# Moving a depthwise convolution's taps, a modulation product and some operands between the engines of a fused two-layer decoder trunk

## The chip, the cores and the metric

One core of a Trainium2 chip runs the whole network as one program. The metric is the time on the device in microseconds (us); the time of a kernel is the median of several runs. One further execution of each kernel is recorded by the hardware profiler. The engines are named as in the profile: PE multiplies matrices (PEld is its weight load), DVE is the vector engine, ACT the scalar engine, POOL the GpSimd engine, and SP only issues DMAs.

## What is computed

Sequence length S = 1024, width D = 1024, feed-forward width F = 2816, two layers, all in fp32. Layer 0 mixes tokens with a convolution module, layer 1 with a pooling mixer; each is followed by a gated feed-forward block.

```python
c_act = silu(c)
for i in range(2):
    mod = c_act @ ada_w[i] + ada_b[i]                # six vectors of 1024
    sh_m, sc_m, g_m, sh_f, sc_f, g_f = split(mod, 6)
    h = rms_norm(x, norm_mix_g[i]) * (1 + sc_m) + sh_m
    y = conformer_conv(h) if i == 0 else multiscale_pool(h)
    x = x + (1 + g_m) * y
    h = rms_norm(x, norm_ffn_g[i]) * (1 + sc_f) + sh_f
    x = x + (1 + g_f) * ((silu(h @ w_gate) * (h @ w_up)) @ w_down)
return rms_norm(x, final_g)

def conformer_conv(h):
    a, g = split(h @ w1 + b1, 2)
    u = a * sigmoid(g)
    u = causal_depthwise_conv(u, w_dw, width=31) + b_dw
    return silu(layer_norm(u)) @ w2 + b2
```

## The kernel before

Activations lie transposed: channels on the 128 partitions (eight tiles of 128 channels, p or k = 0 to 7), tokens along the free axis, in two chunks A and B of 512 tokens. Each product is taken from three matmuls of 512 columns on split operands (`products`, L410): high times high, high times low, low times high, so a weight and an activation exist as a "hi" and a "lo" tile. The low part of a streamed weight is made in `load_weight` (L394): SP loads the raw tile of 512 KB, ACT writes the high part and a negated copy (two instructions on 128x1024), and POOL issues a second DMA of the same bytes that adds into the negated copy (L406). Five weight buffers and three raw buffers rotate.

PE's instructions run in the order of the code. The order on the other engines is made by a scheduler when the program is built; on the chip each engine and each DMA queue runs its list strictly in that order. Work beside the products is cut into generators (`Task`, `Taps`) that `pace()` moves forward at every twelfth or twenty-fourth matmul, as far as a model clock for each engine allows; the prices in `PRICES` set how many steps DVE ("V") and POOL ("G") get. `finish()` and `need()` move what is left of a task at once and stand for the places where the next products need its result.

Stages of layer 0, in PE's order:

- "first": the products of the first four tiles of w1 for chunk A, tile by tile of the input, while the first norm is made. For this DVE computes `sh_m` and `sc_m` as dot products of 1024 elements (`ada_dot`, L308), two for each of the eight tiles.
- The other tiles of w1 for A (outputs "a" and "g") and for B. `conv_glu` (L565) makes u from a pair of outputs, and u's last 30 columns are kept in `uhalo` for B. Meanwhile the taps of the convolution for A run: for tiles 0 to 6 a `Taps` task (L636) deals its 31 taps out, DVE taking multiply-adds into a PSUM bank "ca", POOL taking adds into "pa" of products "pr" that ACT makes. Tile 7 goes over PE: `pe_taps` (L617) multiplies by 128x128 diagonal matrices, one for each tap, split into hi and lo, which ACT makes from an identity (`diagonals`, L605; 62 instructions); its u is split by `split_u`, into two slots of chunk B's pool of u tiles.
- In the same stretch `ada_columns` (L352) computes four modulation vectors (`g_m`, `sh_f`, `sc_f`, `g_f`; j = 2 to 5) on PE, 32 rounds, one for each loaded tile "adaw" of 512 KB from `adan`; a round is eight matmul records and comes at a pace point, at least LOAD["load"] = 2.5 us of the model clock behind the round before. Two buffers hold these tiles, filled from SP's queue.
- `finish` of A's taps, then two tiles of w1 for B (HOLD_LN = 2) beside the layer norm of A (`layer_norm_silu`, L706: sum over tiles, mean on PE, centring, squares, variance, then vhi and vlo).
- "y": the products with w2 for A (`conv_out`, eight tiles, 192 matmuls), the sum of squares of the new x, one more tile of w1 for B, then the norm of the feed-forward block for A, which needs `sc_f` and `sh_f`.
- The feed-forward blocks ("gate", "up", "dn"), with B's taps beside A's block, and layer 1 in the same manner.

A's activations (hhi, hlo, vhi, vlo, mxhi, mxlo) lie in sixteen slots of 512 columns, got by `slot` (L232).

Of the kernel before, what the change touches and what calls it, by code (L numbers as in the profile page):

```python
# [9 lines left out]
F32 = mybir.dt.float32  # L10
# [6 lines left out]
P = 128  # L17
# [27 lines left out]
PE_TAPS = (7,)  # L45
DIAGS = 8
OUT_B = 3
LOAD = {"load": 2.5, "slow": 18.0, "next": 4.0}
# [20 lines left out]
class Chunk:  # L69
# [9 lines left out]
    "G": {"": (0.15, 0.0021, 0.06), "tensor_scalar": (0.2, 0.0009, 0.06), "memset": (0.06, 0.0, 0.0), "tensor_copy": (0.2, 0.0, 0.0)},  # L79
    "S": {"": (0.1, 0.00083, 0.09)},  # L80
}

# [25 lines left out]
def trunk(ctx, tc, xT, c, vec, ada, adan, w1f, w1, w2, wgu, wdn, wpl, out):  # L108
# [51 lines left out]
    def nm(s):  # L160
        uid[0] += 1
        return f"{s}_{uid[0]}"
# [69 lines left out]
    def slot(ch, name, dt=F32R):  # L232

        return slots.tile([P, ch.n], dt, tag=f"s{ch.i}", name=nm(name))
# [223 lines left out]
    class Squares:  # L458


        def __init__(self, ch, psum=False):
            self.ch, self.acc, self.psum = ch, None, psum

        def add(self, k):
            ch = self.ch
            if self.acc is None:
                self.acc = bank("acc") if self.psum else temp(ch.n, "acc", 2)
                S_.activation(self.acc, x[ch.i][k], AF.Square)
            else:
                sq = temp(ch.n)  # L470
                S_.activation(sq, x[ch.i][k], AF.Square)
                was = self.acc
                if self.psum and k == KT - 1:
                    self.acc = temp(ch.n, "acc", 2)
                V_.tensor_tensor(self.acc, was, sq, op=ADD)
# [89 lines left out]
    def conv_glu(ch, p, ba, bg):  # L565
        u = st["u", ch.i, p]
        sg = temp(ch.n)
        S_.activation(sg, bg, AF.Sigmoid, bias=V("conv_b1", KT + p))
        V_.scalar_tensor_tensor(u[:, HALO:], ba, V("conv_b1", p), sg, op0=ADD, op1=MUL)
        if ch.i == 0:  # L570
            G_.tensor_copy(uhalo[:, p, :], u[:, ch.n : ch.n + HALO])

    def conv_in(*todo):

        def emit(take):
            got = {}
            for each in todo:
                if each is None:
                    finish(T["norm_b"])
                    continue  # L580
                ch, p = each
                conv_u(ch, p)
                wts = got.setdefault(p, [])
                b = [bank("a"), bank("g")]
                for i in range(2):
                    if len(wts) == i:
                        wts.append(take())
                    for k in range(KT):
# [4 lines left out]
                if ch.i == 0 and p in PE_TAPS:  # L593
                    split_u(p)
                elif ch.i == 0:
                    T["taps", 0, p] = Taps(A, p)
        tiles = list(dict.fromkeys(e[1] for e in todo if e))
        unit(emit, *[w1[p, i] for p in tiles for i in range(2)])

    def split_u(p):  # L600

        u = st["u", 0, p]
        hi, lo = st["us", p] = [wslot(B, name, F32R) for name in ("uhi", "ulo")]
        S_.copy(hi, u)
        either(A.width).tensor_tensor(lo, u, hi.bitcast(F32), op=SUB)  # L605

    def diagonals(p, js):

        def make():
            wt = wts.tile([P, 2, D], F32R, tag="w", name=nm("diag"))  # L610
            for i, j in enumerate(js):
                for part, w in enumerate((vecs[:, _COLS["conv_wdw"] + j * KT + p :][:, :1], wlow[:, j, p - PE_TAPS[0] : p - PE_TAPS[0] + 1])):
                    S_.activation(wt[:, part, i * P : i * P + P], ident, AF.Copy, scale=w)
            return wt
        return make

    def pe_taps(p):  # L617

        groups = [range(j, min(j + DIAGS, CW)) for j in range(0, CW, DIAGS)]
        us = []  # L620
        for i, js in enumerate(groups):
            def emit(take, i=i, js=js):
                if i == 0:
                    st["tap", p] = bank("tap")
                b, wt = st["tap", p], take()
                for q, j in enumerate(js):
                    products(b, wt, q, [v[:, j : j + A.n] for v in st["us", p]], j == 0, j == CW - 1)
                    if q % 4 == 3:
                        pace()
                if i == len(groups) - 1:  # L630
                    S_.activation(st["u", 0, p][:, HALO:], b, AF.Identity, bias=V("conv_bdw", p))
                    st["taps", 0][p] = True
            us.append((emit, diagonals(p, js)))
        return us

    class Taps:  # L636
# [5 lines left out]
        def __init__(self, ch, p):  # L642
            self.ch, self.p, self.done, self.urgent = ch, p, False, False
            self.next, self.acc, self.part, self.busy = 0, None, None, 0
            tasks.append(self)

        def step(self, e):
# [6 lines left out]
            if self.next < CW - 1:  # L654
                if e == "V" and self.acc is None and sum(isinstance(t, Taps) and t.acc is not None for t in tasks) >= 2:
                    return False
                if e == "G":
                    if self.acc is None and self.part is None and sum(isinstance(t, Taps) and t.part is not None for t in tasks) >= 2:
                        return False
                    if self.next >= CW - 3:  # L660
                        return False
# [21 lines left out]
            if e != "V":  # L683
                return False
            if self.part is not None:
                V_.tensor_tensor(self.acc, self.part, self.acc, op=ADD)
            d = u[:, HALO : HALO + n]
            V_.scalar_tensor_tensor(d, d, w(CW - 1), self.acc, op0=MUL, op1=ADD)
# [17 lines left out]
    def layer_norm_silu(ch):  # L706
# [293 lines left out]
    rstd_last = V_.last.ins.name  # L1000
    h_a = st["h", 0] = [(slot(A, "hhi"), slot(A, "hlo")) for _ in range(KT)]
    fb = [bank("first") for _ in range(BANKS)] + [spare_bank("first") for _ in range(2 * FIRST - BANKS)]
    for k in range(KT + 1):
        if k < KT:
            if k:
                w = ada_pair(k)
                ada_dot(w[:, 1], 0, 1, k)
                tc.add_manual_dep(V_.last.ins, t_last, edge, reason="behind the first norm")
        if k > 0:
            dot = V_.last.ins.name  # L1010
            V_.scalar_tensor_tensor(h_a[k - 1][1], t, mod[:, k - 1 : k], h_a[k - 1][0].bitcast(F32), op0=ADD, op1=SUB)
            if k < KT:
                tc.add_manual_dep(V_.last.ins, dot, edge, reason="the scalar engine's part takes that long")
            for q in range(2 * FIRST):
                products(fb[q], wt, q, h_a[k - 1], k == 1, k == KT)
        if k < KT:
            ada_dot(w[:, 0], 0, 0, k)
            if k == 0:
                tc.add_manual_dep(V_.last.ins, rstd_last, edge, reason="behind the first norm")
# [10 lines left out]

    wdw = V("conv_wdw", 0, CW * KT).rearrange("p (j k) -> p j k", k=KT)[:, :, PE_TAPS[0] : PE_TAPS[-1] + 1]
    whigh = cst.tile([P, CW, len(PE_TAPS)], F32R, name="whigh")
    wlow = cst.tile([P, CW, len(PE_TAPS)], F32, name="wlow")
    S_.copy(whigh, wdw)
    G_.tensor_tensor(wlow, wdw, whigh.bitcast(F32), op=SUB)
# [38 lines left out]
    def ada_first(take):  # L1074
        T["ada", 0] = Task(ada_columns((2, 3, 4, 5)), False, 0)
        T["ada", 0].free = True
    unit(ada_first)
    def norm_first():
        squares = Squares(B, True)
        for k in range(KT):  # L1080
            squares.add(k)
            yield
# [16 lines left out]
    unit(lambda take: finish(*(T["taps", 0, p] for p in range(KT) if p not in PE_TAPS)))  # L1099
# [9 lines left out]
    unit(lambda take: stretch.__setitem__(0, STRETCH))  # L1109
# [97 lines left out]
```

## Time and profile before

| | us |
|---|---|
| median of 3 runs (lowest, highest) | 1869.29 (1868.43, 1871.13) |
| the profiled execution | 1870.55 |
| span of its trace | 1868.8 |
| PE busy | 1819.3 (97%) |
| PE weight loads busy | 1479.8 (79%) |
| DVE busy | 970.0 (52%) |
| ACT busy | 982.7 (53%) |
| POOL busy | 626.7 (34%) |
| DMA | 382.31 MB, mean 205 GB/s |

Times inside the trace count from the start of its span. A busy share is an average over very different stages: "first" ends at 69 us, the convolution stage with the product "y" runs up to about 335 us, and the rest is feed-forward. The chain of waits names for each moment the instruction that set the end; the windows view gives, for stretches of 20 us, each engine's busy time with the number of its instructions in brackets, then the clock that PE was granted (1.00 is full speed), the busy share of the DMA engines and the rate in GB/s.

### The profile page before, as it was taken

Reading aid. Unit: us, or ns where it says so; the run is one execution under the profiler, and the core shown is the slowest. Engines: PE = TensorE matmul, PEld = TensorE weight load, DVE = VectorE, ACT = ScalarE, POOL = GpSimd, SP = SyncE. Lnnn points to the kernel's source line nnn. Section 1 sums busy time; section 2 is a strip of 40 time slices with the busy share of each in tenths; the row PEclk is TensorE's granted clock in tenths of the full one; section 3 lists DMA queues with packets and bytes.
Section 4 is the critical chain, followed back from the end, with each engine's and each line's share of the span. In section 5 each row is a group of like instructions: output and inputs, shape, how many; then the busy total and the mean of one; then the engine's idle time right before and its main releaser. Section 6 shows DMA issues by size and latency. Waiting matters only on the chain.

```text
span 1868.8 us, 22009 instructions
## 1 busy us (share of the span) xinstructions
PE 1819.3 (97%) x8197; PEld 1479.8 (79%) x8197; DVE 970.0 (52%) x1489; ACT 982.7 (53%) x1302; POOL 626.7 (34%) x670
## 2 busy tenths in 40 slices
PE   6899989999999999999999999999999999999997
PEld 5666678888888888877888888888888888888886
DVE  8699753998876236486633223644432243322225
ACT  3566766866656454554553445644534454444443
POOL 4387721878753211273211111421111111111111
PEclk9999989999999999999999999999999999999998
DMA  7968558898897988999887887878888879788782
GB/s 281 289 189 225 150 121 203 205 227 221 210 235 187 237 221 194 262 266 271 232 207 180 198 198 182 193 180 208 188 187 193 195 175 250 178 202 198 181 196 68
DMA packets 106844, 382.31 MB, mean 205 GB/s; under 512 B 11633, under 2 KB 13809, under 8 KB 106738
## 3 DMA queue, kind: packets, MB, share of 16 engines
q0 software_dynamic: 43488, 158.35, 46.1%
q1 hardware_dynamic: 62160, 221.51, 34.4%
q8 instruction: 64, 1.05, 0.2%
q10 hardware_dynamic: 1090, 1.05, 0.2%
q14 instruction: 42, 0.34, 0.1%
HBM read 376.67 MB, written 4.19 MB: 204 GB/s over the span
## 4 chain that ended last, share of the span: by engine, by line
PE 89%; DMA 5%; DVE 4%; POOL 1%; issue 1%; ACT 0%; SPq 0%; DVEq 0%; POOLq 0%
PE gate L124 24%; PE dn L124 24%; PE up L124 24%; PE y L124 6%; PE a L124 3%; PE g L124 3%; PE first L124 2%; DMA adaw<-in_adan_dram 2%; DMA adaw<-in_ada_dram 2%; DVE adaw L102 1%; DVE acc L102 1%; PE ada L124 1%; DVE t L102 1%; PE tap L124 1%; PE rstd L124 1%
## 5 line engine op out<-in xcount | busy, mean ns | idle before, releaser
L102 ACT CAST w<-raw 128x1024 fp32r<-128x1024 f32 x312 | 325.9, 1045 | 509.3 <-issue 300.4
L124 PE MATMUL gate<-hhi,w 128*128 128x512 f32 x1408 | 451.2, 390 | 1.5 <-DVE x L102 1.4
L124 PE MATMUL up<-hhi,w 128*128 128x512 f32 x1408 | 451.4, 390 | 0.0
L124 PE MATMUL dn<-ghi,w 128*128 128x512 f32 (+1 forms) x1440 | 446.0, 387 | 1.7 <-DMA w<-in_wdn_dram 1.7
L406 POOL DMA_DIRECT2D w<-in_wgu_dram x176 | 154.7, 879 | 759.4 <-ACT w L102 739.9
L102 DVE SCALAR_TENSOR_TENSOR x<-dn,gains,x 128x512 f32<-128x512 f32 (+1 forms) x360 | 261.4, 735 | 113.6 <-PE dn L124 113.3
L102 ACT ACTIVATE w<-raw 128x1024 fp32r<-128x1024 f32 x302 | 318.7, 1055 | 0.0
L124 PEld LDWEIGHTS dn<-ghi,w 128*128 128x128 f32 x1440 | 267.8, 187 | 60.0 <-DMA w<-in_wdn_dram 2.2
L124 PEld LDWEIGHTS gate<-hhi,w 128*128 128x128 f32 x1408 | 264.3, 188 | 57.9 <-DVE x L102 2.6
L124 PEld LDWEIGHTS up<-hhi,w 128*128 128x128 f32 x1408 | 264.3, 188 | 54.8
L102 DVE TENSOR_TENSOR t<-t,up 128x512 f32<-128x512 f32 x86 | 59.0, 686 | 475.1 <-PE up L124 446.7
L124 PE MATMUL dn<-glo,w 128*128 128x512 f32 (+1 forms) x720 | 278.5, 387 | 0.0
L124 PE MATMUL gate<-hlo,w 128*128 128x512 f32 x704 | 274.3, 390 | 1.4 <-DVE hlo L102 1.4
L124 PE MATMUL up<-hlo,w 128*128 128x512 f32 x704 | 273.9, 389 | 0.0
L102 POOL TENSOR_TENSOR pa<-pa,pr 128x512 f32<-128x512 f32 x165 | 232.0, 1496 | 27.2 <-ACT pr L102 24.4
L102 DVE SCALAR_TENSOR_TENSOR ca<-u,vecs,ca 128x512 f32<-128x512 f32 x255 | 176.1, 746 | 0.7
L124 PEld LDWEIGHTS dn<-glo,w 128*128 128x128 f32 x720 | 135.1, 188 | 28.3 <-issue 0.2
L124 PEld LDWEIGHTS gate<-hlo,w 128*128 128x128 f32 x704 | 132.1, 188 | 29.6 <-DVE hlo L102 2.3
L406 POOL DMA_DIRECT2D w<-in_wdn_dram x88 | 78.5, 892 | 225.8 <-ACT w L102 223.8
L124 PEld LDWEIGHTS up<-hlo,w 128*128 128x128 f32 x704 | 132.1, 188 | 27.2
L102 ACT ACTIVATE t<-gate 128x512 f32<-128x512 f32 x86 | 51.2, 595 | 156.9 <-PE gate L124 151.7
L102 DVE SCALAR_TENSOR_TENSOR adaw<-adaw,cact 128x1024 f32<-128x1024 f32 x64 | 108.2, 1693 | 42.6 <-DMA adaw<-in_ada_dram 42.6
(139 smaller groups left out, 1799.1 us busy)
## 6 DMA issues: line engine op xcount, KB each, us to landing
raw<-in_wgu_dram SPq DMA_DIRECT2D x176, 512.0 KB, 6.9
w<-in_wgu_dram POOLq DMA_DIRECT2D x176, 512.0 KB, 8.0
raw<-in_wdn_dram SPq DMA_DIRECT2D x88, 512.0 KB, 5.4
w<-in_wdn_dram POOLq DMA_DIRECT2D x88, 512.0 KB, 9.0
adaw<-in_ada_dram SPq DMA_DIRECT2D x48, 512.0 KB, 7.4
raw<-in_w_dram SPq DMA_DIRECT2D x36, 512.0 KB, 5.2
w<-in_w_dram POOLq DMA_DIRECT2D x34, 512.0 KB, 8.4
adaw<-in_adan_dram SPq DMA_DIRECT2D x32, 512.0 KB, 5.5
```

The source lines that it names most:

```text
L102: self.last = self.order(getattr(self.eng, name)(out, *args, **kw))
L124: last_mm[0] = nc.tensor.matmul(out, lhsT, rhs, start=start, stop=stop).ins.name
L406: order(nc.gpsimd.dma_start(low if len(src.shape) == 2 else low.rearrange("p (a b) -> p a b", a=src.shape[1]), src, accum_op=ADD))
```

## The change

Taps. `PE_TAPS` becomes a map: tile 7 has all 31 taps on PE, and tile 6 has its last 8 there; the other 23 stay with DVE and POOL, and its `Taps` task ends by adding the PSUM bank that PE filled. The diagonals are no longer made by ACT. They are laid out on the host in DRAM (`wdg`), five tiles of 128x1024 (eight taps each), and come through `load_weight` like every other weight. The splits of u now lie in A's slots, with two zero columns ahead, and a tap moves its shift partly to the output: a tap at distance s writes from column 2*(s//2) on, so it has fewer columns. For that each slot of A has 514 columns, and every tile that `slot` returns starts at its third column.

Modulation. `ada_columns` keeps j = 2 and 3 (16 rounds), paced by 4.0 in place of 2.5. `sc_f` and `g_f` (j = 4 and 5) become dot products on DVE, two tasks of eight, started when the layer norm of A is done, that is ahead of "y", each paced by 3.5; `sc_f` has to be finished behind "y".

Operands and order. The running sum of A's layer norm lies in PSUM until its last step, and so does the first tile's t in "first". Tile 7's u is made in place in PSUM and split from there. `uhalo` is written by DVE (ACT for tile 7) in place of POOL. In "first" the low part of tile 0 comes ahead of the dots of tile 1. The squares for B's first norm are issued one step ahead of their sums. POOL's price per element in the planner goes from 0.0021 to 0.0026 until the feed-forward block starts.

```diff
-PE_TAPS = (7,)
+PE_TAPS = {6: 8, 7: CW}
-LOAD = {"load": 2.5, "slow": 18.0, "next": 4.0}
+LOAD = {"load": 4.0, "slow": 18.0, "next": 4.0, "dots": 3.5}
-    "G": {"": (0.15, 0.0021, 0.06), ...
+    "G": {"": (0.15, 0.0026, 0.06), ...
+def tap_groups(p):
+    todo = list(range(CW - 1, CW - 1 - PE_TAPS[p], -1))
+    return [todo[i : i + DIAGS] for i in range(0, len(todo), DIAGS)]
...
     def slot(ch, name, dt=F32R):
-        return slots.tile([P, ch.n], dt, tag=f"s{ch.i}", name=nm(name))
+        return slot_after(ch, name, dt)[:, 2 - 2 * ch.i :]
+    def slot_after(ch, name, dt=F32R):
+        return slots.tile([P, ch.n + 2 - 2 * ch.i], dt, tag=f"s{ch.i}", name=nm(name))
...
-    def ada_task(l, js):
+    def ada_task(l, js, pause=None):
...
-                yield "next" if lax[0] else "slow"
+                yield pause or ("next" if lax[0] else "slow")
...
+        if ch.i == 0 and PE_TAPS.get(p) == CW:
+            V_.scalar_tensor_tensor(ba, ba, V("conv_b1", p), sg, op0=ADD, op1=MUL)
+            hi, lo = st["us", p] = [slot_after(A, name) for name in ("uhi", "ulo")]
+            for part in (hi, lo):
+                G_.memset(part[:, :2].bitcast(F32), 0.0)
+            S_.copy(hi[:, 2:], ba)
+            V_.tensor_tensor(lo[:, 2:], ba, hi[:, 2:].bitcast(F32), op=SUB)
+            S_.copy(uhalo[:, p, :], ba[:, ch.n - HALO :])
+            return
         V_.scalar_tensor_tensor(u[:, HALO:], ba, V("conv_b1", p), sg, op0=ADD, op1=MUL)
         if ch.i == 0:
-            G_.tensor_copy(uhalo[:, p, :], u[:, ch.n : ch.n + HALO])
+            V_.scalar_tensor_tensor(uhalo[:, p, :], ba[:, ch.n - HALO :], V("conv_b1", p), sg[:, ch.n - HALO :], op0=ADD, op1=MUL)
...
     def split_u(p):
-        u = st["u", 0, p]
-        hi, lo = st["us", p] = [wslot(B, name, F32R) for name in ("uhi", "ulo")]
+        u = st["u", 0, p][:, HALO - 2 :]
+        hi, lo = st["us", p] = [slot_after(A, name) for name in ("uhi", "ulo")]
         S_.copy(hi, u)
-        either(A.width).tensor_tensor(lo, u, hi.bitcast(F32), op=SUB)
-    def diagonals(p, js):
...
-                    S_.activation(wt[:, part, i * P : i * P + P], ident, AF.Copy, scale=w)
+        either(A.n).tensor_tensor(lo, u, hi.bitcast(F32), op=SUB)
     def pe_taps(p):
...
-                    products(b, wt, q, [v[:, j : j + A.n] for v in st["us", p]], j == 0, j == CW - 1)
+                    o = (CW - 1 - j) // 2 * 2
+                    i0 = 2 - (CW - 1 - j) % 2
+                    products(b[:, o:], wt, q, [v[:, i0 : i0 + A.n - o] for v in st["us", p]], j == CW - 1, j == CW - PE_TAPS[p])
...
+                    else:
+                        T["taps", 0, p].other = b
-            us.append((emit, diagonals(p, js)))
+            us.append((emit, wdg[sum(len(tap_groups(q)) for q in PE_TAPS if q < p) + i]))
...
-            if e != "V":
+            if e != "V" or self.awaits and self.other is None:
                 return False
...
+            if self.awaits:
+                if self.part is not None:
+                    V_.tensor_tensor(d, self.part, self.acc, op=ADD)
...
+                V_.tensor_tensor(d, d, self.other, op=ADD)
...
-        acc = temp(n, "acc", 2)
+        acc = None
...
+            was = vs[0] if k == 1 else acc
+            if k == KT - 1 or ch.i and acc is None:
+                acc = temp(n, "acc", 2)
+            elif acc is None:
+                acc = bank("acc")
-            V_.tensor_tensor(acc, vs[0] if k == 1 else acc, vs[k], op=ADD)
+            V_.tensor_tensor(acc, was, vs[k], op=ADD)
...
+            if k == 1:
+                tc.add_manual_dep(dots[0], low_last, edge, reason="behind the first values")
...
-            t = temp(A.n)
+            t = temp(A.n) if k else first_t
...
-        T["ada", 0] = Task(ada_columns((2, 3, 4, 5)), False, 0)
+        T["ada", 0] = Task(ada_columns((2, 3)), False, 0)
...
     need("ln_a")
+    unit(lambda take: [T.__setitem__(("ada", 0, j), ada_task(0, (j,), "dots")) for j in (5, 4)])
     sq_a = Squares(A)
     conv_out(A, sq_a, lambda take: [now(columns_done(*g)) for g in held_back])
+    unit(lambda take: finish(T["ada", 0, 4]))
     unit(lambda take: T.__setitem__("norm_a", Task(norm(A, 0, True, ("h", 0), squares=sq_a), True)))
```

More of the change, by code (lines that the diff above doesn't have):

```diff
@@ L107, in trunk @@
 @with_exitstack
-def trunk(ctx, tc, xT, c, vec, ada, adan, w1f, w1, w2, wgu, wdn, wpl, out):
+def trunk(ctx, tc, xT, c, vec, ada, adan, w1f, w1, wdg, w2, wgu, wdn, wpl, out):
     nc = tc.nc
@@ L1007, in trunk @@
                 ada_dot(w[:, 1], 0, 1, k)
-                tc.add_manual_dep(V_.last.ins, t_last, edge, reason="behind the first norm")
+                if k > 1:
+                    tc.add_manual_dep(V_.last.ins, t_last, edge, reason="behind the first norm")
+                dots = [V_.last.ins]
         if k > 0:
@@ L1079, in norm_first @@
         squares = Squares(B, True)
-        for k in range(KT):
-            squares.add(k)
+        for k in range(KT + 1):
+            if k < KT:
+                squares.square(k)
+            if k > 1:
+                squares.sum(k == KT)
             yield
@@ L1098, in trunk @@
     unit(lambda take: finish(T["ada", 0]))
-    unit(lambda take: finish(*(T["taps", 0, p] for p in range(KT) if p not in PE_TAPS)))
+    unit(lambda take: finish(*(T["taps", 0, p] for p in range(KT) if PE_TAPS.get(p, 0) < CW)))
     for p in rest[len(rest) - HOLD - HOLD_LN : len(rest) - HOLD]:
@@ L1182 @@
     up = np.stack([tiles(np.asarray(ffn_w_up)[l], NF) for l in range(DEPTH)])
+    taps = np.asarray(conv_wdw)[0].reshape(CW, KT, P)
+    groups = [(p, js) for p in sorted(PE_TAPS) for js in tap_groups(p)]
+    diag = np.zeros((len(groups), P, DIAGS, P), np.float32)
+    for i, (p, js) in enumerate(groups):
+        for q, j in enumerate(js):
+            diag[i, range(P), q, range(P)] = taps[j, p]
     arrays = {
```

84 lines of the change are left out of this document (44 added, 40 removed).

## The prediction

> **What bounds the kernel now.** I read the page first, then the windows of 20 us, then the waits and the chain, last the groups of DVE, ACT and POOL inside the convolution stage. The page:
>
> ```profile
> span 1868.8 us, 22009 instructions
> ...
> PE   6899989999999999999999999999999999999997
> ...
> q0 software_dynamic: 43488, 158.35, 46.1%
> q1 hardware_dynamic: 62160, 221.51, 34.4%
> ```
>
> The second row is PE's busy tenths in 40 slices: it is busy throughout, so most of the span is its own matmuls, and a change pays where slices fall under 9, or where matmuls go or grow. The last two rows are the DMA queues with their packets, MB and share of the DMA engines' time. The windows show these places (busy us and instructions of PE, PEld, DVE, ACT, POOL, then clock, DMA share, GB/s):
>
> ```profile
> 80.00:100.00 20.00, 15.67 (x77) 10.34 (x78) 10.91 (x18) 10.34 (x16) 9.15 (x9) 0.83 0.97 274
> ...
> 160.00:180.00 20.00, 17.13 (x93) 11.28 (x93) 15.70 (x20) 10.20 (x16) 14.67 (x13) 0.91 0.87 224
> ...
> 220.00:240.00 20.00, 14.32 (x60) 10.20 (x59) 9.99 (x14) 9.20 (x13) 11.06 (x12) 0.90 0.80 189
> 240.00:260.00 20.00, 18.59 (x77) 14.97 (x76) 14.80 (x34) 12.85 (x18) 4.45 (x6) 0.84 0.31 64
> ...
> 300.00:320.00 20.00, 20.00 (x94) 16.70 (x93) 5.96 (x16) 11.31 (x14) 2.92 (x4) 1.00 0.88 199
> ```
>
> And PE's waits (us in total, times, longest):
>
> ```profile
> PE ada L124 <- DMA adaw<-in_adan_dram: 10.6, 6, 5.2
> ...
> PE mean L124 <- DVE acc L102: 4.7, 1, 4.7
> ```
>
> Full speed is about 90 matmuls per 20 us (fifth row). Behind each idle piece the clock is below 1.00: 0.83 and 0.91 cost up to (0.17 + 0.09) x 20 = 5.2 us behind the waits for "adaw" tiles, 0.90 and 0.84 likewise 5.2 us around the layer norm. The chain (start, duration, what) gives the prices:
>
> ```profile
> 140.67 2.95 PE g L124 x12
> 143.62 0.57 PE ada L124 x8
> ...
> 147.14 2.72 PE a L124 x12
> ...
> 236.91 2.09 PE mean L124 x2
> ...
> 268.28 43.52 PE y L124 x192
> ...
> 320.86 0.91 PE rstd L124 x8
> ```
>
> Twelve matmuls take 2.72 us (226.7 ns each), but 2.95 behind a round "ada", which itself is 0.57: a round costs PE 0.80. The layer norm's mean comes at 236.9, "y" starts at 268.3, it lasts 43.5, and the norm behind it has its rstd at 320.9 + 0.9 = 321.8.
>
> **(a) The start of "first".** DVE's list puts two dots ahead of the first low part:
>
> ```profile
> 18.81 0.74 DVE L102 SCALAR_TENSOR_TENSOR t<-x,gains,rstd 128x512 f32<-128x512 f32 x1
> 19.47 2.71 DVE L102 SCALAR_TENSOR_TENSOR adaw<-adaw,cact 128x1024 f32<-128x1024 f32 x1
> ...
> 22.42 0.73 DVE L102 SCALAR_TENSOR_TENSOR hlo<-t,mod,hhi 128x512 fp32r<-128x512 f32 x1
> ```
>
> and PE's list then has
>
> ```profile
> 23.21 0.79 PE L124 MATMUL first<-hlo,w 128*128 128x512 f32 x1 [2.05 <-DVE hlo L102]
> ```
>
> The x2 row is 2.71 us. With the dots behind, the low part waits only for ACT's hhi and can come at 20.4 instead of 22.4; both dots now stand ahead of tile 1's t, but PE has 24 matmuls (5.4 us) of tile 0 to cover them. I take -1.5; bounds -2.0 and 0, since DVE is nearly saturated behind it. t in PSUM, the reordered squares and `uhalo` move work of under a microsecond between engines beside PE and get nothing; uncovered, eight writes of 30 columns would cost DVE some 2 us.
>
> **(b) PE's work up to the end of the taps.** Sixteen of 32 rounds go: 16 x 0.80 = -12.8. Eight taps add 24 matmuls. A tap's price comes from these two rows of PE's timeline; between them start 30 matmuls:
>
> ```profile
> 224.89 0.63 PE L124 MATMUL tap<-uhi,diag 128*128 128x512 f32 x2
> ...
> 231.86 0.39 PE L124 MATMUL tap<-uhi,diag 128*128 128x512 f32 x1
> ```
>
> (231.86 - 224.89)/30 = 0.232, so +5.6; the shortened outputs take back 3 x 474 columns, 0.6: +5.0. Of the waits for "adaw" (10.6 us in 6) and their clock (I take 3.5 of the 5.2), those behind 150 us (the windows from 160 and from 220) lie in the half of the rounds that is removed, and the remaining loads are asked for about half as often, so I leave 2 us of them: -12.1. Bounds: -14 (all gone) and -6 (the early ones stay, as first loads still meet the weights of the next tiles). Sum (b): -19.9.
>
> **(c) The layer norm of A.** PE gets to its mean some 20 us sooner, so A's taps have to be done sooner too. In the convolution stage (60 to 236 us) these groups count:
>
> ```profile
> L102 DVE SCALAR_TENSOR_TENSOR ca<-u,vecs,ca 128x512 f32<-128x512 f32 x121 | 83.7, 747 | 0.6
> L102 DVE TENSOR_TENSOR acc<-acc,u 128x512 f32<-128x512 f32 x5 | 7.2, 1445 | 0.1
> L102 DVE TENSOR_TENSOR acc<-acc,t 128x512 f32<-128x512 f32 x7 | 4.9, 698 | 10.5 <-ACT t L102 10.3
> L102 DVE TENSOR_TENSOR ca<-pa,ca 128x512 f32<-128x512 f32 x7 | 4.8, 688 | 10.6 <-POOL pa L102 10.6
> L102 POOL TENSOR_TENSOR pa<-pa,pr 128x512 f32<-128x512 f32 x75 | 100.6, 1434 | 17.9 <-ACT pr L102 17.0
> L406 POOL DMA_DIRECT2D w<-in_w_dram x17 | 15.8, 928 | 24.0 <-ACT w L102 21.4 <-issue 2.2 <-POOL pa L102 0.4
> L102 ACT CAST w<-raw 128x1024 fp32r<-128x1024 f32 x18 | 18.8, 1045 | 26.2 <-PE g L124 11.8 <-PE a L124 7.9 <-PE tap L124 6.4
> L102 ACT ACTIVATE w<-raw 128x1024 fp32r<-128x1024 f32 x17 | 18.0, 1058 | 0.0
> L102 ACT ACTIVATE diag<-ident,vecs 128x128 fp32r<-128x128 f32 x31 | 12.0, 388 | 0.3 <-PE a L124 0.3
> L102 ACT ACTIVATE diag<-ident,wlow 128x128 fp32r<-128x128 f32 x31 | 12.0, 388 | 0.0
> ```
>
> DVE waits 10.6 us for POOL's sums and 10.5 for ACT's squares; POOL waits 17.9, nearly all for "pr" of ACT, and 24.0 for ACT's w ahead of its DMA issues. ACT spends 2 x 12.0 us on 62 diagonal pieces, and "pr" waits in the same list. The 62 pieces go. Five weights come in: on ACT 5 x (1.045 + 1.058) = 10.5 us, net -13.5; on POOL five issues of 0.93, +4.6, each of which may also wait for ACT's w with POOL's adds queued behind it; on SP five raw loads, between the others. In the planner a POOL add now costs 0.15 + 512 x 0.0026 = 1.48 us, near the measured 1.434 instead of 1.23, so POOL gets some 12 adds fewer than its 75 (17 us less), and DVE, with eight taps fewer to share, about four more (3 us). The sum in PSUM should bring the five "acc" additions from 1.445 to about 0.70: -3.7 on DVE. Without DVE's waits for POOL and ACT (21 us) and with the work above the taps would end some 25 us sooner, the mean standing at about 212 where it stands at 236.9. So PE's wait for the mean (4.7 us), the one ahead of the variance and their slow clock (10 us together) should not grow: I take -6. Bounds: -10, and +12 if the taps move by only 8 us. The split of tile 6 waits for A's last products to free slots; it is needed only at "tap", two tiles later.
>
> **(d) Sixteen dots beside "y".** DVE is nearly free there (5.96 of 20), so the dots themselves (two took 2.71 us in the row of (a)) are covered. The loads are not: DMA is at 0.88. By the queue rows a weight takes 0.524/158.35 of 46.1% for its second DMA and 0.524/221.51 of 34.4% for its raw one, of 1868.8 us: 2.85 + 1.52 = 4.37 us of all engines for each 5.44 of PE, and a pair of dots adds 3.04. Together 7.4 per 5.44: DMA becomes the bound. Landing times:
>
> ```profile
> adaw<-in_ada_dram SPq DMA_DIRECT2D x48, 512.0 KB, 7.4
> w<-in_w_dram POOLq DMA_DIRECT2D x34, 512.0 KB, 8.4
> 831.19 14.43 DMA adaw<-in_ada_dram
> ```
>
> Two buffers mean two dots for each landing. DMA is emptier just ahead of "y" (0.31 at 240 to 260), so I estimate four to six dots in its first third, then two for each 8 to 9 us (7.4 and a dot): the last of sixteen at about 62 us behind the start of "y", when rstd is ready at 321.8 - 268.3 = 53.5. `sc_f` needs the last or next to last: +7 (a short idle costs clock too). Late next: SP's list is in order, so raw weights wait behind a load without a buffer, and the first gate and up weights come late by about the same; that lies in the same wait. Bounds: 0, if the planned pace holds (a pair per 5.44 us ends at 44), and +30, if landings stay near 14.4.
>
> [...]
>
> **(e) A's slots.** Every operand in a slot of A now starts two columns behind its slot's start, and the slots are 514 columns apart. That looks free, but PE's time per matmul differs between operands of equal size:
>
> ```profile
> 386.52 5.44 PE up L124 x24
> 391.96 10.99 PE dn L124 x48
> 402.94 5.44 PE gate L124 x24
> ```
>
> "gate" takes 5.44/24 = 226.7 ns, "dn" 10.99/48 = 229.0, from tiles of 542 columns read at their start, and the taps, which start anywhere in such a tile, 232.3. A's slots feed 2736 matmuls: first 192, a and g 192, y 192, gate and up 2 x 1056, the pooling mixer's y 48. Nothing hides them. Bounds: 0 at gate's price, 2736 x 5.6 ns = 15.3 at the taps'; between, 6.3 at dn's. I take 15.3, since only the taps start off their tile's start.
>
> [...]
>
> **Sum.** -1.5 - 19.9 - 6 + 7 + 15.3 = -5.1. The span is 1868.8, the profiled execution about 1.8 above it, and that one 1.3 above the median of 1869.3, so 1869.3 - 5.1 = 1864.
>
> **Rivals.** 1, the slots and the dots cost nothing: -27.4, 1842. For it: gate's own price, and a pace that ends at 44 us; against: the tap rows and DMA at 0.88. 2, slower: `sc_f` arrives late. The place is the wait for the norm behind "y"; if landings stay near 14.4 us, two dots for each, sixteen need 115 us; even if the last third speeds up once PE stands still, the norm waits some 30 us: -5.1 + 23 = +18, 1887. It decides against the change from a wait of about 12 us on. For it: two loads in flight only, SP's order; against: the median of 7.4. 3, the taps end only 8 us sooner, because five more POOL issues wait for ACT with its adds behind them: (c) is +7 to +12 instead of -6, total about +10, 1879. For it: POOL's 24.0 us; against: ACT's relief. 4, PE's taps of tile 6 relieve nobody, as DVE's last addition waits for PE's bank: worth eight taps at most, inside (c).
>
> **How the numbers follow.** A measurement of this kernel tells about 0.2% (3.7 us) from no change. Forecast 0.45, of which 0.33 faster, 0.07 within, 0.05 slower; rival 1, with what lies between it and the forecast, 0.22, faster; rival 2 0.16, slower; rival 3 0.14, of which 0.02 faster, 0.01 within, 0.11 slower; anything else 0.03, 0.01 faster, 0.02 slower. Together faster 0.58, within 0.08, slower 0.34. The forecast's own range is 1852 to 1873; out to rival 1 and into rival 2 it is 1843 to 1883.
>
> **What would show it.** (a) the first low matmul near 21 instead of 23.2. (b) sixteen rounds of "ada", few waits for adan, the last tap matmul near 211 instead of 232. (c) "y" starting near 240; if DVE or POOL still ends its last tap past 225, (c) is wrong. (d) the feed-forward norm starting more than 54 us behind y's start, its last dot being what it waits for; no wait there makes it wrong. (e) gate on A at 5.5 to 5.6 us per 24 while B stays at 5.44; 5.44 for both makes it wrong. A loss inside the feed-forward blocks other than (e) would be outside this prediction.

## The result and the profile after

The changed kernel takes 1870.99 us (median of 12 runs, 1867.6 to 1876.35) where the kernel before takes 1869.2 beside it (12 runs, 1865.73 to 1872.33): a ratio of 1.0009, with a 95% interval of 0.9999 to 1.0019. No difference can be told. The forecast of 1864 lay 7 us too low; 1871 is inside its own range and the wide one, but the gain that was forecast isn't there, and "no difference" had been given a chance of 0.08 only.

Two rows of PE's timeline in the kernel before show where the span can be cut: the first matmul of "y" for A and the first "dn" (start and duration in us, engine, line, operation, output and inputs, shapes).

```profile
268.11 0.39 PE L124 MATMUL y<-vhi,w 128*128 128x512 f32 x1
...
359.05 0.39 PE L124 MATMUL dn<-ghi,w 128*128 128x512 f32 x1
```

The same two of the changed kernel, whose span is 1869.4 us:

```profile
238.76 0.49 PE L131 MATMUL y<-vhi,w 128*128 128x512 f32 x1
...
346.16 0.39 PE L131 MATMUL dn<-ghi,w 128*128 128x512 f32 x1
```

| us | before | after | difference |
|---|---|---|---|
| to the first matmul of "y" | 268.1 | 238.8 | -29.4 |
| from there to the first "dn" | 90.9 | 107.4 | +16.5 |
| from there to the end of the span | 1509.8 | 1523.2 | +13.5 |
| span | 1868.8 | 1869.4 | +0.6 |

So the convolution stage won 29 us, and two other stretches gave them back. The waits of PE after the change (us in total, times, longest) show the first line of the table: the 10.6 us for "adaw" and the 4.7 for the mean are nearly gone.

```profile
PE ada L131 <- DMA adaw<-in_adan_dram: 2.2, 3, 1.8
...
PE mean L131 <- DVE acc L109: 1.7, 1, 1.7
```

The windows show the second: at 280 to 320 PE, which was full beside "y" before, is idle for 9 us and its clock is at 0.86 and 0.89.

```profile
260.00:280.00 20.00, 20.00 (x87) 16.20 (x86) 8.73 (x14) 10.72 (x14) 3.36 (x4) 1.00 1.05 306
280.00:300.00 20.00, 14.53 (x62) 11.86 (x61) 8.84 (x15) 8.72 (x11) 2.74 (x4) 0.86 0.99 288
300.00:320.00 20.00, 16.24 (x63) 11.90 (x63) 16.63 (x35) 9.13 (x13) 3.68 (x9) 0.89 0.63 187
```

DVE's timeline there, where a bracket gives the idle time and what ended it, names the cause:

```profile
293.36 1.22 DVE L109 SCALAR_TENSOR_TENSOR adaw<-adaw,cact 128x1024 f32<-128x1024 f32 x1 [1.81 <-DMA adaw<-in_ada_dram]
...
294.51 0.75 DVE L109 SCALAR_TENSOR_TENSOR x<-t,gains,x 128x512 f32<-128x512 f32 x1
...
300.47 1.22 DVE L109 SCALAR_TENSOR_TENSOR adaw<-adaw,cact 128x1024 f32<-128x1024 f32 x1 [3.47 <-DMA adaw<-in_ada_dram]
...
301.62 0.17 DVE L109 TENSOR_SCALAR var<-var 128x4 f32<-128x4 f32 x1
...
307.67 1.23 DVE L109 SCALAR_TENSOR_TENSOR adaw<-adaw,cact 128x1024 f32<-128x1024 f32 x1 [1.93 <-DMA adaw<-in_ada_dram]
...
308.82 2.72 DVE L109 SCALAR_TENSOR_TENSOR t<-x,gains,rstd 128x512 f32<-128x512 f32 x4
```

The norm's first "t" starts at once behind the sixteenth dot, and that dot had to wait for its load. The rows above it show more than the forecast had seen: DVE ran its list in order, so an update of x (294.51) and the variance's first step (301.62) also stand behind a dot that waits for DMA, 1.81 and 3.47 us; ACT had made the update's t by 291.4, 3.1 us before. The groups of the stretch from 240 to 310 us, first DVE's dots (busy us, mean ns, then DVE's idle time ahead of them), then the DMA issues (KB, median us from issue to landing):

```profile
L109 DVE SCALAR_TENSOR_TENSOR adaw<-adaw,cact 128x1024 f32<-128x1024 f32 x16 | 19.6, 1223 | 26.3 <-DMA adaw<-in_ada_dram 26.3
```

```profile
adaw<-in_ada_dram SPq DMA_DIRECT2D x14, 512.0 KB, 7.4
```

The dots cost DVE 19.6 us; their loads cost it 26.3 us of waiting. The third line of the table is seen in the chain of waits: "gate" on a slot of A takes 5.61 us, on a slot of B, far behind, 5.44 as before.

```profile
323.89 5.61 PE gate L131 x24
...
346.32 10.99 PE dn L131 x48
...
1478.97 5.44 PE gate L131 x24
```

### The profile page after: what moved, and what is told of

The parts are those of the page before. It is cut to its first block, busy times and chain, and to the rows that moved or that the text cites. A ratio compares the mean times of both kernels' runs of the same rounds, so it can differ in the third digit from the quotient of the medians.

```text
span 1869.4 us, 21783 instructions
## 1 busy us (share of the span) xinstructions
PE 1826.0 (98%) x8085; PEld 1481.9 (79%) x8085; DVE 990.9 (53%) x1528; ACT 968.0 (52%) x1240; POOL 614.8 (33%) x662
## 3 DMA queue, kind: packets, MB, share of 16 engines
q8 instruction: 64, 1.05, 0.2%
q10 hardware_dynamic: 1090, 1.05, 0.2%
## 4 chain that ended last, share of the span: by engine, by line
PE 82%; DVE 10%; DMA 6%; issue 1%; ACT 1%; SPq 0%; POOL 0%; DVEq 0%
PE gate L131 24%; PE up L131 24%; PE dn L131 24%; DMA adaw<-in_ada_dram 5%; DVE ca L109 4%; PE y L131 4%; PE first L131 3%; DVE adaw L109 1%; DVE acc L109 1%; PE g L131 1%; PE a L131 1%; DVE x L109 1%; DVE t L109 1%; DMA adaw<-in_adan_dram 1%; DVE hlo L109 1%
## 5 line engine op out<-in xcount | busy, mean ns | idle before, releaser
L109 ACT CAST w<-raw 128x1024 fp32r<-128x1024 f32 x317 | 331.0, 1044 | 508.2 <-issue 303.8
L109 ACT ACTIVATE w<-raw 128x1024 fp32r<-128x1024 f32 x307 | 323.9, 1055 | 0.0
L109 POOL TENSOR_TENSOR pa<-pa,pr 128x512 f32<-128x512 f32 x156 | 222.9, 1545 | 13.6 <-ACT pr L109 10.9
L109 DVE SCALAR_TENSOR_TENSOR adaw<-adaw,cact 128x1024 f32<-128x1024 f32 x80 | 118.9, 1488 | 65.1 <-DMA adaw<-in_ada_dram 65.0
```

The costliest lines, as they stand in the source:

```text
L109: self.last = self.order(getattr(self.eng, name)(out, *args, **kw))
```

## The experiments

Each time is a median, and each ratio is against the kernel before on the same chip, with a 95% interval; the changed kernel stands at 1.0009 on that scale.

### Where the operands start

**A's slots back (e1_slots_back).** The changed kernel with

```diff
-        return slot_after(ch, name, dt)[:, 2 - 2 * ch.i :]
+        return slots.tile([P, ch.n], dt, tag=f"s{ch.i}", name=nm(name))
...
     def slot_after(ch, name, dt=F32R):
...
-        return slots.tile([P, ch.n + 2 - 2 * ch.i], dt, tag=f"s{ch.i}", name=nm(name))
+        return wslot(B, name, dt)[:, : ch.n + 2]
```

> The changed kernel, with A's slots 512 columns wide again and read from their first column; the three-part splits of u at the second product take two of B's u buffers instead. Theory: PE's price per matmul follows the start of the moving operand, and 2736 matmuls of A pay 5 to 6.4 ns each for it: this run is 13 to 17 us below the changed kernel's 1871, at 1854 to 1858, and gate and up take 5.44 us per 24 in A as in B. Rival (the slots are innocent; A's matmuls are slower for what streams beside them): gate and up of A stay at 5.6 us and the time at 1871.

**The slots alone (e2_before_shifted).** The kernel before with

```diff
-        return slots.tile([P, ch.n], dt, tag=f"s{ch.i}", name=nm(name))
+        return slots.tile([P, ch.n + 2 * (1 - ch.i)], dt, tag=f"s{ch.i}", name=nm(name))[:, 2 * (1 - ch.i) :]
```

> The kernel before, with nothing changed but A's slots: 514 columns wide, every operand read from the third column. Theory: the start alone costs 2736 matmuls 5 to 6.4 ns each, so 13 to 17 us more than 1869, 1882 to 1886, with A's gate and up at 5.6 us per 24. Rival (the slots are innocent): 1869 and 5.44 us.

Measured: 1858.4 us for the first (0.9940, 0.9921 to 0.9959) and 1887.45 for the second (1.0092, 1.0064 to 1.0121). The chain of the first, then of the second, in A's feed-forward block of layer 0:

```profile
395.31 5.44 PE gate L131 x24
```

```profile
384.30 5.59 PE gate L124 x24
```

Both stand within 1.5 us of what the theory gave: the shift costs 17.8 us by itself and its removal brings 12.6. The removal brings less: in its profiled execution, which at 1862.64 us is the slowest of its four, "y" starts some 4 us later, with the splits of u in buffers of B; what delays it wasn't taken apart. Behind the first "dn" it needs 1509.2 us, as the kernel before does.

**Matmuls by themselves (e10_starts).**

```python
    def batch(name, at, wat=0, count=96):
        b = ps.tile([P, 512], F32, tag="b", name=name)
        o, wo = (at - BASE) // 4 % 64, wat // 4
        for i in range(count):
            k = wo + i % 8 * P
            nc.tensor.matmul(b, stay[:, k : k + P], move[:, o : o + 512], start=i == 0, stop=i == count - 1)
```

> Nothing but matmuls: batches of 96, each matmul with its own 128x128 weight and a moving operand of 128x512, started at 0, 8, 16, 32, 48, 64, 72, 96, 104, 128, 136, 160, 192, 200, 224 and 248 bytes behind a multiple of 256 bytes, the list once upwards and once downwards; then with the weights moved by 8, 64 and 128 bytes. No other engine works and nothing of the reference is computed. Theory: the start alone sets the price, with 64 at 227 ns, 192 at 232 ns and starts off a multiple of 64 at 232 to 237 ns as in the changed kernel, and the weights' start changes nothing. Rival (the price comes from other engines' traffic into the same memory): all batches at one price within 1 ns.

Measured: 983.34 us for the whole program, one run. The list of starts runs once up and once down ("up", "dn"), then three starts with moved weights ("stay"). In this program the weights start at 128 behind a multiple of 256 bytes, unless moved. The chain, 96 matmuls to a row; the last letter of "up" gives the operand's start (f 64, g 72, j 128, k 136, m 192, n 200), that of "stay" the weights' move (x by 8, y by 64, z by 128), the letter ahead of it the operand's start again:

```profile
165.41 22.39 PE up_f L1234 x96
...
255.00 21.78 PE up_j L1234 x96
276.79 22.41 PE up_k L1234 x96
...
321.59 21.97 PE up_m L1234 x96
343.57 22.61 PE up_n L1234 x96
...
813.53 21.97 PE stayfz L1234 x96
835.50 22.10 PE staygx L1234 x96
...
924.76 21.77 PE staymy L1234 x96
946.53 22.41 PE staymz L1234 x96
```

A start at 64, which is the fast one in the kernel, is slow here: 22.39/96 = 233.2 ns. Fast is 128, with 226.9 ns, where the weights start too; and when the weights are moved to 192, an operand at 192 becomes the fast one (staymy, 226.8), while with the weights at 0 it takes 233.4 (staymz). 64 bytes behind the weights costs a third of that (228.9, up_m and stayfz), 8 bytes all of it (233.4, up_k), and 72 bytes is the worst place (235.5, up_n). So the theory was right that traffic of other engines isn't needed, and wrong in the rest: the fast place is the one where the moving operand starts where the weights do, modulo 256 bytes. Distance alone does not set the price of the other places: 64 bytes ahead of the weights it is 233.2 ns in up_f, but 230.2 in staygx, where the weights are moved by 8.

**The weights moved instead (e12_weights_moved).** The kernel before with

```diff
+    gap = ctx.enter_context(tc.tile_pool(name="gap", bufs=1))
+    gap.tile([P, 32], F32, name="gap")
     wts = ctx.enter_context(tc.tile_pool(name="wts", bufs=W_BUFS))
```

> The kernel before, with 128 bytes left free ahead of the weight tiles and nothing else touched: A's and B's slots stay where they were, at 64 behind a multiple of 256 bytes, while the weights move from 64 to 192. Theory (from the matmul batches: fast only where the moving operand and the weights start at the same place in 256 bytes): all 5472 matmuls that read slots of A and B become slow by 4.8 to 6.4 ns, the two halves of dn's change places: 26 to 35 us more than 1869, 1895 to 1904, with gate at 5.6 us per 24 in A and B. Rival (the moving operand's own place decides): 1869 and 5.44 us.

Measured: 1899.1 us (1.0164, 1.0149 to 1.0179), with no slot moved (the raw and temporary tiles, which lie behind the weights, move along): 30.8 us for 5472 matmuls, 5.6 ns each. Its chain:

```profile
386.56 5.57 PE gate L124 x24
...
397.71 11.01 PE dn L124 x48
```

The program's addresses fit: in the kernel before weights and slots all start at 64; of 2160 "dn" matmuls half read a tile at 64 and half one at 192, since those tiles are 2176 bytes apart (from start to start those at 192 mostly take 232 to 234 ns there, those at 64 226 or 227), which is why "dn" took 229.0 and stays at 11.0 us here, where its halves change places.

### What the norm waits for

**sc_f first (e3_scale_first), and with the slots (e4_both).** The changed kernel with

```diff
-    unit(lambda take: [T.__setitem__(("ada", 0, j), ada_task(0, (j,), "dots")) for j in (5, 4)])
+    unit(lambda take: T.__setitem__(("ada", 0, 4), ada_task(0, (4,), "dots")))
...
     unit(lambda take: finish(T["ada", 0, 4]))
+    unit(lambda take: T.__setitem__(("ada", 0, 5), ada_task(0, (5,), "dots")))
...
     for i, (e, ws) in enumerate(fa):
+        if i == 2:
+            unit(lambda take: finish(T["ada", 0, 5]))
```

> The changed kernel, with the same sixteen dots in another order: sc_f's eight stand first beside y, and g_f's eight start behind them and are finished ahead of the first dn. Theory: the feed-forward norm of A waits for the last of sixteen dots, and with eight it waits for none: 12 to 16 us below 1871, at 1855 to 1859, with about 91 us from the start of y to the first dn as before the change (107 in the changed kernel). Rival (DMA is the bound there, and the weights of gate and up come late whatever the dots do): the time stays within 4 us of 1871, as the wait only moves to the first gates.

> The changed kernel with both edits: A's slots read from their first column, and sc_f's dots ahead of g_f's. Theory: the two losses are at different places and add up: 25 to 31 us below 1871, at 1840 to 1846, which is what the earlier start of y gives by itself. Rival (one of the two hides the other, or the gain of the convolution stage is lost again further on): no better than the better one of the two alone, about 1855.

Measured: 1881.28 us (1.0054, 1.0035 to 1.0073) and 1864.26 (0.9970, 0.9957 to 0.9984): 8 and 6 us slower than without the reordering. The theory fell in both, and in the first its rival too, which had the time unchanged; in the second the rival holds, that the two are no better than the slots alone. The norm's wait did go: "y" to the first "dn" takes 96.9 us. But PE then waits in "dn", by its waits from 320 to 370 us:

```profile
PE dn L131 <- DVE x L109: 7.5, 1, 7.5
PE dn L131 <- DVE t L109: 7.4, 1, 7.4
```

and the timeline and DVE's groups there show why:

```profile
337.42 5.33 POOL L109 TENSOR_TENSOR pa<-pa,pr 128x512 f32<-128x512 f32 x4
...
338.21 9.03 DVE L109 SCALAR_TENSOR_TENSOR adaw<-adaw,cact 128x1024 f32<-128x1024 f32 x1 [0.52 <-DMA adaw<-in_ada_dram]
...
347.17 3.38 DVE L109 SCALAR_TENSOR_TENSOR ca<-u,vecs,ca 128x512 f32<-128x512 f32 x5
...
351.71 0.68 DVE L109 TENSOR_TENSOR t<-t,up 128x512 f32<-128x512 f32 x1
...
358.02 2.27 DVE L109 SCALAR_TENSOR_TENSOR adaw<-adaw,cact 128x1024 f32<-128x1024 f32 x1
...
362.04 4.04 DVE L109 SCALAR_TENSOR_TENSOR x<-dn,gains,x 128x512 f32<-128x512 f32 x6 [1.74 <-POOL gains L109]
```

```profile
L109 DVE SCALAR_TENSOR_TENSOR adaw<-adaw,cact 128x1024 f32<-128x1024 f32 x9 | 22.2, 2470 | 2.0 <-DMA adaw<-in_ada_dram 1.9
```

A dot that takes 1.2 us beside "y" takes 2.5 on average beside the feed-forward block, 1.6 without the one that takes 9.0; the "t" that PE needs stands behind that one. Moved there, the dots lie beside POOL's adds for B's taps, the one of 9.0 us beside the row of four from 337.42. The wait for x has another reason: the updates of x need `g_f` itself, whose last dot ends only at 360.3, and the gains that POOL makes from it.

**No dots (e5_no_dots).** In place of the task for the dots:

```diff
+    def bias_only(take):
+        for j in (5, 4):
+            V_.memset(mod[:, j * KT : (j + 1) * KT], 0.0)
+            ada_post(0, j, 0, KT, G_)
+            ada_done.add((0, j))
+    unit(bias_only)
```

> The changed kernel with the sixteen dots beside y and their loads left out: layer 0's sc_f and g_f are made from the bias alone, so that part of the modulation isn't computed. Theory: nothing else makes the feed-forward norm of A late, so the stretch from the start of y to the first dn falls from 107.4 us to about 91 as before the change, and the time by 13 to 18 us from 1871, to 1853 to 1858. Rival (the weights of gate and up come late in that stretch whatever the dots do): the stretch stays above 100 us and the time within 5 us of 1871.

**Dots without their loads (e6_no_loads).** The sixteen dots go over two loaded tiles in turn:

```diff
...
-                ada_dot(ws.pop(0), l, j, k)
-                if i + ADA_BUFS < len(todo):
+                ada_dot(ws[0], l, j, k)
+                ws.append(ws.pop(0)) if reuse else ws.pop(0)
+                if not reuse and i + ADA_BUFS < len(todo):
...
```

> The changed kernel with all sixteen dots in place, but with two loads for them instead of sixteen: the dots go on over the same two buffers, so sc_f and g_f are not the reference's. Theory: what is late is the landing of the loads, two at a time; the dots' own 16 x 1.2 = 20 us fit into DVE's idle time beside y: the same time as with no dots at all, 1853 to 1858. Rival (the dots' own time, and the updates of x that stand behind them on DVE, make the norm late): 1866 to 1872.

Measured: 1859.14 (0.9937, 0.9922 to 0.9953) and 1859.47 (0.9940, 0.9925 to 0.9955), a little short of the theory's -13 to -18 and far from both rivals. In the version without dots the two rows are

```profile
238.92 0.49 PE L131 MATMUL y<-vhi,w 128*128 128x512 f32 x1
...
334.03 0.39 PE L131 MATMUL dn<-ghi,w 128*128 128x512 f32 x1
```

95.1 us apart, so the dots cost 107.4 - 95.1 = 12.3 us of the 16.5; and nearly all of that is their loads, since sixteen dots without loads cost nothing that can be measured. Of the other 4.2 us, 288 matmuls on A's slots (192 of "y", 96 of "gate" and "up") at 6.3 ns make 1.8. Some 2.1 of the remaining 2.4 lie in the first 24 matmuls of "y": they take 7.69 us here and 5.44 in the kernel before, as PE now reaches "y" while its vhi and vlo are still being made. The second of them:

```profile
240.08 0.50 PE L131 MATMUL y<-vlo,w 128*128 128x512 f32 x1 [0.67 <-POOL vlo L109]
```

**An earlier start (e11_early).** e1_slots_back with one task for all sixteen dots, started behind the last tap:

```diff
-LOAD = {"load": 4.0, "slow": 18.0, "next": 4.0, "dots": 3.5}
+LOAD = {"load": 4.0, "slow": 18.0, "next": 4.0, "dots": 3.5, "pair": 9.0}
...
-                yield pause or ("next" if lax[0] else "slow")
+                yield ("pair" if i in (0, 2) else "dots") if pause else ("next" if lax[0] else "slow")
...
+    unit(lambda take: T.__setitem__(("ada", 0, 4), ada_task(0, (4, 5), "dots")))
     for p in rest[len(rest) - HOLD - HOLD_LN : len(rest) - HOLD]:
```

> The changed kernel with A's slots read from their first column, and the sixteen dots as one task (sc_f's eight, then g_f's) that is started right behind PE's last tap, some 25 us ahead of y, so that at most two loads are asked for at a time; the first and third dot are planned 9 us behind their loads. Theory: the loads are what is late, so with a start 25 us sooner the last dot is no longer behind the norm: 8 to 14 us below the 1858 of the version with the slots alone, at 1844 to 1850, with y's start where it was. Rival (a dot that waits for its load holds the layer norm of A, which stands behind it in DVE's list): y starts 5 us or more later and the time is 1858 or more.

Measured: 1861.43 us (0.9966, 0.9955 to 0.9976), no gain over e1_slots_back (0.9940). "y" starts no later (241.1 against 242.9), so the rival's reason is wrong as well. From 240 to 320 us its dots and loads are

```profile
L109 DVE SCALAR_TENSOR_TENSOR adaw<-adaw,cact x15: 1216/1220/1229, 240.9 to 315.0; 128x1024 f32<-128x1024 f32 x15
...
DMA to landing us min/median/max: 3.2/7.4/13.8
```

Only one dot was done ahead of 240; fifteen follow in 75 us, 5 us each, the last one at 316, later than the 308.9 of the changed kernel. In this run the pace of the loads, asked for one behind the other over two buffers, set the end, and not the start. It doesn't tell what a start with more dots ahead of "y" would bring.

### What left PE

**All rounds back (e7_pe_again), and half (e8_half).** The first is the changed kernel with `ada_columns((2, 3, 4, 5))` and no dots; the second e1_slots_back with `ada_columns((2, 3, 4))` and dots for g_f alone.

> The changed kernel with all four vectors made by PE's 32 rounds again and no dots beside y; diagonal weights, taps, sums in PSUM and slots as changed. Theory: sixteen rounds bring back 16 x 0.80 = 12.8 us on PE and some 3 to 6 of waits for their loads, and the feed-forward norm gives back 13 to 18: the two nearly cancel, 1868 to 1877; the dots gained nothing as they stand. Rival (the rounds cost PE nothing that the layer norm doesn't wait for anyway): 1853 to 1858; rival (the loads of sixteen more rounds stall PE much more than before, beside the loads of the diagonal weights): above 1880.

> The changed kernel with A's slots read from their first column, sc_f made by PE's rounds (24 in all), and only g_f's eight dots beside y, finished before the norm is planned. Theory: eight loads land before y is done, so the norm waits for none of them; against the version with A's slots alone (1858) eight rounds cost 6.4 to 9 us and the wait of 13 to 18 goes: 1847 to 1854. Rival (eight dots make the norm late too, or the rounds cost what the dots did): 1858 or more.

Measured: 1902.44 (1.0165, 1.0149 to 1.0181) and 1867.22 (0.9990, 0.9980 to 0.9999). Both theories fell; for the first the rival of over 1880 holds, for the second the one of 1858 or more. Windows and waits of the first show a hole behind the mean:

```profile
220.00:240.00 20.00, 7.64 (x65) 1.79 (x64) 7.93 (x12) 6.84 (x11) 3.18 (x3) 0.59 0.69 217
240.00:260.00 20.00, 13.16 (x73) 7.86 (x68) 2.00 (x12) 0.11 (x1) 0.00 (x0) 0.62 0.30 102
```

```profile
PE ada L131 <- DMA adaw<-in_adan_dram: 19.2, 10, 6.5
PE adac L131 <- ACT t L109: 5.7, 1, 5.7
```

Twelve of the 32 rounds did not fit ahead of the mean and are run one behind the other, each waiting for its load, before the layer norm goes on; in the half version it is four. The change also raised the price LOAD["load"] from 2.5 to 4.0 us of the model clock, so a round comes every 6 to 8 us instead of every 3.5. The run thus shows what 32 rounds cost at the new pace, not what sixteen cost before; 32 rounds at 2.5 were not tried.

**No taps of tile 6 on PE (e9_no_taps).** The changed kernel with `PE_TAPS = {7: CW}`.

> The changed kernel with tile 6's eight taps back on DVE and POOL, so without its split and its 24 matmuls on PE. Theory (DVE is at 20.00 of 20 us from 120 to 200 and ends the taps): PE is done about 5 us sooner, DVE and POOL 4 to 6 us later, so PE waits for the mean 8 to 10 us instead of 1.7 and the time rises by 3 to 6 us from 1871, to 1874 to 1877. Rival (PE's taps relieve nobody, the sum of the taps waits for PE's bank): 5 us less, 1866.

Measured: 1878.21 (1.0052, 1.0032 to 1.0073), 8 us slower than the changed kernel. PE's wait for the mean:

```profile
PE mean L131 <- DVE acc L109: 15.7, 1, 15.7
```

The direction is the theory's, the size larger: PE waits 15.7 us where 8 to 10 were expected. The eight taps are worth their 24 matmuls.

## Which steps of the forecast held, and where its sum went wrong

- **(a) to (c), the start of "y".** Forecast -27.4 us, measured -29.4; with the 384 matmuls on A's slots that lie ahead of "y", which the sum had counted under (e) and which cost some 2.5 us, it is -31.9. Some 2.1 us of it are lost again at once, as "y" now starts ahead of its operands. PE's first low matmul comes at 20.89, where 21 was expected. (The row of 2.71 us, which the forecast reads as two dots, is one, x1; the usual dot takes 1.2. No term of the sum goes by it.) The waits for "adaw" fell from 10.6 to 2.2 us, and the mean stands at 216.9 instead of 236.9: 20 us sooner, not the 25 that (c) gave the taps and not the 8 of rival 3. Without PE's eight taps of tile 6 it stands at 224.0 (e9_no_taps), so 7 of these 20 us hang on them, and rival 4, that they relieve nobody, is wrong. What the loaded diagonals, the sum in PSUM and the dealing brought was not taken apart.
- **(d), the dots: the step that was mis-sized.** That the dots' loads cost the time is shown (1870.99 falls to 1859 without dots, or without their loads), and the last wait is the one that was forecast, the norm's for the last dot. The forecast put the last dot 62 us behind the start of "y" and the loss at 7 us; it ends 308.9 - 238.8 = 70.1 us behind it and costs 12.3. Four to six dots were expected in the first third of "y" (14.5 us); the fifth is done after 18.6 us. From there it should have been 4.25 us a dot, and the other eleven took 51.5 us, 4.7 each: of the waits for loads in the chain between 255 and 294 us, three of four are 8.7 to 9.0 us, where a landing of 7.4 was counted. What was missed is that the updates of x, their squares and the variance stand behind waiting dots in DVE's list, so that rstd is late as well. The changed kernel, then the version without dots:

```profile
305.89 1.13 PE L131 MATMUL rstd<-ident,col 128*128 128x128 f32 x8 [1.64 <-DVE col L109]
```

```profile
295.01 1.05 PE L131 MATMUL rstd<-ident,col 128*128 128x128 f32 x8
```

It is ready 68.3 us behind the start of "y" instead of 57.1 (the forecast had 53.5). By these rows the norm would be some 11 us late even if it didn't need the last dot, whose wait adds 1.8 us; no run takes the two apart. Rival 2, with a wait of 30 us, is wrong in size.
- **(e), A's slots.** Forecast +15.3, measured 17.8 by themselves (e2_before_shifted). The upper bound, the taps' 232.3 ns, was too low: starts 8 and 72 bytes behind the weights, two of the eight places that A's slots take at 2080 bytes from one to the next, take 233.4 and 235.5 (e10_starts). The price came out by luck, for a wrong reason: not the start inside the tile counts, but the place relative to the weights ("gate" at 5.57 us per 24 in e12_weights_moved, where no slot moved).
- **The sum.** -31.9 + 12.3 + 2.4 + 17.8 = +0.6, the difference of the spans. Against -5.1: 4.5 us more gain ahead of "y", 5.3 and 2.4 (mostly the slow start of "y") more loss in (d)'s stretch, 2.5 more in (e). That it closes to the tenth is luck: the interval of the 17.8 alone is 12 to 23 us. Rival 1 needed both losses at zero; with the slots back and no other repair 1858.4 is reached, the best version measured, 0.6% below the kernel before. The two repairs of (d) that were tried, e3_scale_first and e11_early, brought nothing.

## What to carry to other kernels

A gain on the critical path was kept here only as far as what was taken off it had another free path with all its parts: the dots had free time on DVE (1859.47 us without their loads, 1859.14 without dots), their loads, with a DMA share of 1.05 and 0.99 from 260 to 300 us, had none and cost nearly all of the 12.3 us. In DVE's in-order list a load that was late held everything behind it (26.3 us of waiting from 240 to 310 us), so it is the wait, not the 1.2 us of the instruction, that has to be placed. And an operand's start was not free (17.8 us for A's slots): before padding a tile by a few bytes, compare the price per matmul on both tiles in the chain of waits, and keep weights and moving operands at the same place modulo 256 bytes, the fast one in all these runs (226.7 to 226.9 ns, and up to 235.5 elsewhere).

## What was not expected of the hardware

**Two operands, one place.** 96 matmuls of 128x512 in fp32r take 21.8 us where moving operand and weights start at the same place modulo 256 bytes and up to 22.6 elsewhere, 3.8% more, with nothing else running; 128 bytes ahead of the weight tiles cost the kernel before 30.8 us. Moving either of the two changes the price: the operand from 128 to 64, with the weights at 128, from 226.9 to 233.2 ns a matmul (up_j, up_f); the weights from 192 to 0, with the operand at 192, from 226.8 to 233.4 (staymy, staymz). Why, no run here shows.

**A long addition beside POOL's adds.** In the changed kernel one addition of two tiles in SBUF took 12.8 us instead of the 0.68 of B's same step at 530.8, beside a row of POOL's adds: it ended at 149.4, 1.5 us behind the seventh of them and inside the eighth. DVE's timeline and POOL's:

```profile
136.65 12.78 DVE L109 TENSOR_TENSOR acc<-u,u 128x512 f32<-128x512 f32 x1
149.34 2.06 DVE L109 SCALAR_TENSOR_TENSOR ca<-u,vecs,ca 128x512 f32<-128x512 f32 x3
```

```profile
137.65 4.35 POOL L109 TENSOR_TENSOR pa<-pa,pr 128x512 f32<-128x512 f32 x3
...
141.99 5.89 POOL L109 TENSOR_TENSOR pa<-pa,pr 128x512 f32<-128x512 f32 x4
...
147.58 2.97 POOL L109 TENSOR_TENSOR pa<-pa,pr 128x512 f32<-128x512 f32 x1
```

The dot of 9.0 us in e3_scale_first, also with two operands in SBUF, lies beside POOL's adds in the same way, while the multiply-adds with one operand in PSUM stay at 0.75 us there (26 of them from 300 to 370 us, with 28 of POOL's adds). That POOL's adds hold DVE is the author's estimate from these rows; no run here takes them away to show it.
